# Reordering the gated merge of a hybrid S5, sparse-attention and SwiGLU block, and splitting its 16 weight pieces earlier

## The chip, the cores and the metric

The kernel runs on one core of a Trainium2 chip. The metric is the device time of one execution in microseconds (us). Its engines in the profile are PE (matmuls), DVE, ACT and POOL (elementwise work), and SP, which issues the transfers; every engine runs its instructions in the order in which they were written for it, and waits for another engine on semaphores.

## The reference

One decoder block over 2048 tokens of width 1024, in float32, cut to what matters here:

```python
h = _rms(x, norm1_g)
u, q, k, v, qi, ki, wi, gates = split(h @ w_in)
y_ssm = _s5_branch(u, ..., w_glu, b_glu)       # 512 wide, ends in a gated linear unit
y_att = _dsa_branch(q, k, v, qi, ki, wi)       # 512 wide: each query attends to its 256 best keys
g_ssm, g_att = split(gates)                    # 1024 wide each
merged = sigmoid(g_ssm) * (y_ssm @ w_proj_ssm) + sigmoid(g_att) * (y_att @ w_proj_attn)
x = x + merged @ w_out
h2 = _rms(x, norm2_g)
x = x + (silu(h2 @ w_ffn_gate) * (h2 @ w_ffn_up)) @ w_ffn_down
```

## The kernel before

Every operand of a large product is held as two parts, hi and lo: hi is the value cast to the matmul's reduced type (fp32r), lo is what the cast lost. `mm3` forms hi·hi, hi·lo and lo·hi, three matmuls for one. Parts are made in two steps: a cast (ACT mostly) and a subtraction (POOL or DVE; a split of a weight piece of 128x1024 is "raw" to "ww" in the trace, hi first).

**Stages.** The projections of phase 1 come first. Then three streams run interleaved: *state* (the S5 scan, then `glu`, its gated linear unit), *attention* (for 4 tiles of 128 queries at a time, a search by bisection for the 256 best keys in `topk`, on DVE and ACT, then scores, softmax and values in `attention`), and *dense* (the rest of the gate projections, "gps" in the trace, then four blocks of 512 tokens). The search for the tiles of the next attention group runs on DVE beside the dense block of the group before. Its result goes out as "bias<-fin", and the group's first matmuls are "lg<-kk,q".

**Who comes next** is settled when the program is written out, not on the chip. Each stream is a generator that yields what it needs next; a planner (`Pace`) holds an estimated clock per engine, adds a cost for each instruction (`note`), and takes the first stream whose need is met by PE's estimated clock (`pick`). `spare` gives an elementwise operation to POOL or DVE, whichever the estimate has free sooner; the additions and subtractions of the merge go through it. So the order on every engine is a fixed list, and an edit of one stream moves instructions of all.

**A dense block** (`block`, 512 tokens) does, in this order:

1. The merge: 16 products of 12 matmuls, one for each of 8 groups of 128 output channels (ct) and each branch (br 0 state space, br 1 attention): "f<-act,ww", with act0 the state-space branch's output and act1 the attention's. In the order ct by ct, both branches beside each other. DVE multiplies each by its gate (`scalar_tensor_tensor`, "g<-g,f"), POOL adds the two branches ("g<-g,g"), ACT and DVE make the parts ("mg<-g", "mg<-g,mg").
2. w_out: "f<-ww,mg", 192 matmuls, each group of 24 over all 8 channel groups of mg; then the residual sum into x1.
3. The norm, transposes ("f<-ident,..."), the up and gate products ("f<-h,ww") and the down products ("f<-wd,at").

**Weights** come through `Rings` in pieces of 128x1024, 4 slots of ring "w". In block 0 a piece is loaded raw, split on the spot and its two parts stored to DRAM ("wc<-ww", 1 MB); blocks 1 to 3 load the stored parts ("ww<-wc", 1 MB). Pieces 0 to 7 hold the two projections, one ct of both branches each; pieces 8 to 15 hold w_out; then come those of the feed-forward part. The merge frees a piece after its second product (`drop`), which lets the next load be issued. Gates come back from DRAM ("g<-gate") two channel groups ahead.

**Start of a block.** Block tb begins when the attention of its four tiles is done (`attended >= 4 * (tb + 1)`), and the first one also not before the gates are done (`gated`). A block takes 3 PSUM banks and borrows spare ones in between (`lend`); the last one, which runs alone, takes 8.

## Time and profile before

| | us |
|---|---|
| median of 3 runs (3353.09 to 3363.12) | 3360.59 |
| profiled execution | 3357.88 |
| its span, from first to last instruction | 3355.8 |
| PE busy | 3171.5 (95%) |
| DVE busy | 2106.4 (63%) |
| ACT busy | 1275.1 (38%) |
| POOL busy | 638.1 (19%) |

In a timeline row come first the start and the length of a run of like instructions, then engine and line, the operation, out<-in by the program's names, the count, and in brackets how long the engine sat idle just before and what ended that. All work of an engine is recorded in one helper, so each row has line 206 and is told apart by its names. A row of the groups has the count, then the shortest, median and longest duration in ns.

### The profile page before, as it was taken

How to read it: one execution, taken by the hardware profiler on the slowest of the kernel's cores; microseconds unless marked ns; L12 is line 12 of the kernel's file. 1: busy time of each engine (PE TensorE's matmuls, PEld its weight loads, DVE VectorE, ACT ScalarE, POOL GpSimd, SP SyncE). 2: the span in 40 equal slices, each digit the busy share in tenths (PEclk: the TensorE clock that was granted, in tenths of full speed). 3: DMA queues.
4: the chain of work that ended last, by engine and by line, in shares of the span. 5: the costliest groups of instructions: out<-in, count | busy, mean ns of one | idle time of the engine just before them, and what ended most of it. 6: DMA issues, size and time to landing. Idle time of an engine off the chain costs nothing. (4 is left out here: it accounts for less than half of the span.)

```text
span 3355.8 us, 42712 instructions
## 1 busy us (share of the span) xinstructions
PE 3171.5 (95%) x15528; PEld 2651.1 (79%) x15528; DVE 2106.4 (63%) x4532; ACT 1275.1 (38%) x2211; POOL 638.1 (19%) x628
## 2 busy tenths in 40 slices
PE   7999989899977999989999999999999999999999
PEld 6988767678755788877778888877888888788887
DVE  6555685555587766688687775876886666422223
ACT  3231544445552444346322443665314444210000
POOL 4323676522223311234100000001000000000000
PEclk9999999999988999999999999999999999999999
DMA  5743333534447775656847324366555332755543
GB/s 184 227 122 109 121 89 108 164 120 142 129 166 268 283 257 196 237 182 225 332 187 262 109 93 166 140 236 242 197 213 182 119 108 88 268 195 219 207 177 149
DMA packets 312961, 605.56 MB, mean 180 GB/s; under 512 B 46352, under 2 KB 194608, under 8 KB 282032
## 3 DMA queue, kind: packets, MB, share of 16 engines
q1 hardware_dynamic: 312752, 602.85, 51.7%
q8 instruction: 122, 2.00, 0.2%
q14 instruction: 87, 0.71, 0.1%
HBM read 434.70 MB, written 166.89 MB: 179 GB/s over the span
## 5 line engine op out<-in xcount | busy, mean ns | idle before, releaser
L206 PE MATMUL f<-h,ww 128*128 128x512 f32 (+1 forms) x4416 | 1013.1, 384 | 1.3 <-DVE h L206 0.8
L206 PEld LDWEIGHTS f<-h,ww 128*128 128x128 f32 x4416 | 803.4, 191 | 156.5 <-DVE h L206 1.8
L206 PE MATMUL f<-wd,at 128*128 128x512 f32 x2112 | 518.2, 397 | 28.7 <-DVE t L206 6.5
L206 PEld LDWEIGHTS f<-wd,at 128*128 128x128 f32 x2112 | 396.3, 191 | 116.5 <-DVE t L206 8.1
L206 PE MATMUL gps<-hT,gw 128*128 128x512 f32 x1536 | 387.5, 403 | 4.6 <-ACT gsg L206 3.2
L206 ACT ACTIVATE jka<-S,tr 128x1920 bf16<-128x1920 f32 (+6 forms) x217 | 305.6, 1408 | 180.5 <-DVE tr L206 128.7
L206 PEld LDWEIGHTS gps<-hT,gw 128*128 128x128 f32 x1536 | 288.3, 193 | 68.5 <-ACT gsg L206 5.2
L206 PE MATMUL mm<-w,hT 128*128 128x512 f32 (+1 forms) x1152 | 282.8, 403 | 10.3 <-DVE hT L206 7.2
L206 DVE TENSOR_TENSOR x<-f,x 128x512 f32<-128x512 f32 x352 | 235.1, 686 | 77.0 <-PE f L206 76.4
L206 PEld LDWEIGHTS mm<-w,hT 128*128 128x128 f32 x1152 | 241.5, 239 | 36.7 <-DVE hT L206 8.6
L206 DVE TENSOR_TENSOR tl<-pt,th 128x512 fp32r<-128x512 f32 (+1 forms) x288 | 183.8, 658 | 120.9 <-ACT th L206 119.8
L206 DVE SCALAR_TENSOR_TENSOR t<-t,f 128x512 f32<-128x512 f32 (+1 forms) x123 | 82.1, 668 | 271.8 <-PE f L206 223.6
L206 ACT CAST th<-pt 128x512 fp32r<-128x512 f32 (+1 forms) x288 | 155.5, 563 | 223.8 <-PE pt L206 220.2
L206 PE MATMUL f<-act,ww 128*128 128x512 f32 x768 | 191.8, 411 | 29.5 <-POOL ww L206 20.4
L206 PEld LDWEIGHTS f<-act,ww 128*128 128x128 f32 x768 | 151.2, 199 | 69.5 <-POOL ww L206 24.2
L206 POOL TENSOR_TENSOR g<-g,g 128x512 f32<-128x512 f32 x31 | 39.8, 1285 | 793.9 <-DVE g L206 793.9
L206 PE MATMUL f<-ww,mg 128*128 128x512 f32 x768 | 180.3, 397 | 10.6 <-ACT ww L206 7.0
L206 ACT ACTIVATE P<-P,m 128x1024 f32<-128x1024 f32 (+7 forms) x192 | 172.3, 900 | 46.9 <-DVE m L206 46.8
L206 PE MATMUL lg<-kk,q 128*128 128x512 f32 (+1 forms) x640 | 183.3, 388 | 3.5 <-DMA kk<-kk 3.5
L206 ACT ACTIVATE t<-f 128x512 f32<-128x512 f32 (+1 forms) x92 | 52.9, 575 | 343.8 <-PE f L206 343.7
L206 PEld LDWEIGHTS f<-ww,mg 128*128 128x128 f32 x768 | 147.2, 192 | 43.2 <-ACT ww L206 7.9
L206 ACT CAST at<-t 128x512 fp32r<-128x512 f32 (+1 forms) x92 | 55.2, 600 | 325.4 <-DVE t L206 325.3
(361 smaller groups left out, 4497.9 us busy)
## 6 DMA issues: line engine op xcount, KB each, us to landing
ww<-wc SPq DMA_DIRECT2D x180, 1024.0 KB, 4.9
wd<-wc SPq DMA_DIRECT2D x66, 1024.0 KB, 7.2
wc<-ww SPq DMA_DIRECT2D x60, 1024.0 KB, 7.5
raw<-in_w_in_dram SPq DMA_DIRECT2D x104, 256.0 KB, 3.4
wc<-wd SPq DMA_DIRECT2D x22, 1024.0 KB, 6.3
x<-in_x_dram SPq DMA_DIRECT2D x32, 512.0 KB, 5.3
gate<-gsg SPq DMA_DIRECT2D x64, 256.0 KB, 2.2
g<-gate SPq DMA_DIRECT2D x64, 256.0 KB, 5.7
```

Of the source, the lines that this page charges most:

```text
L206: return f(*args, **kw)
```

## The change

1. `weights`: pieces 0 to 3 hold two channel groups each of the state-space projection, pieces 4 to 7 of the attention's, in place of both branches of one channel group. The first 16 pieces (8 of the projections, 8 of w_out; `EARLY`) are marked as stored parts in block 0 too.
2. `presplit`, a new stream beside `glu`: it loads these 16 raw pieces, splits them (cast on ACT into "pw", subtraction on POOL) and stores the parts, two raw and two pw buffers. `dense` waits for both streams (`ahead`) where it waited for the gates alone.
3. The merge runs all 8 state-space products first and keeps each, times its gate, in the rows of x1, which are not in use yet; then the 8 attention products, each multiplied by its gate, added to what was kept, and split. The block starts without the attention of its own tiles; the wait for it stands ahead of the attention half. The attention branch is loaded after 6 products if it is ready by then, or after 8. The rows of x are loaded when the attention half has used the kept values. Gates are loaded two channel groups ahead within one branch.
4. Blocks take 3 banks each and borrow 5 when all attention is done; the number of down-weight buffers is fixed inside the block.

On PE, the merge and w_out of block 0, before (the state-space branch is act_9338, the attention branch act_9375):

```order
L206 MATMUL gps<-hT,gw 128x512 x330
L206 MATMUL f<-act_9338,ww 128x512 x24
L206 MATMUL f<-act_9375,ww 128x512 x24
L206 MATMUL f<-act_9338,ww 128x512 x12
L206 MATMUL f<-act_9375,ww 128x512 x12
L206 MATMUL f<-act_9338,ww 128x512 x12
```

and of the change (act_9365 and act_9573):

```order
L207 MATMUL u<-yp,uw_7548 128x256 x12
L207 MATMUL gps<-hT,gw 128x512 x282
L207 MATMUL f<-act_9365,ww 128x512 x96
L207 MATMUL f<-act_9573,ww 128x512 x96
L207 MATMUL f<-ww,mg 128x512 x192
```

The twelve groups of 12 that alternated have become two runs of 96, and 48 matmuls of the gates moved ahead of the last one of `glu` ("u<-yp").

On SP, the transfers from the last gate of the gate projections on, before:

```order
L206 DMA gate_0_164<-gsg 128x512 x2
L206 DMA raw<-in_w_proj_ssm_dram 128x4x128
L206 DMA raw<-in_w_proj_attn_dram 128x4x128
L206 DMA act_9338<-act_182 128x2x512 x4
L206 DMA raw<-in_w_proj_ssm_dram 128x4x128
L206 DMA raw<-in_w_proj_attn_dram 128x4x128
L206 DMA g_9373<-gate_0_134 128x512
L206 DMA act_9375<-att_186 128x2x512 x4
L206 DMA g_9380<-gate_0_136 128x512
```

and the last loads of the state-space half of the change (wc_190 to wc_205 are the stored parts; act_9365 and wc_190 to wc_194 were issued ahead of these rows):

```order
L207 DMA g_9508<-gate_0_144 128x512
L207 DMA ww<-wc_195 128x2048
L207 DMA g_9544<-gate_0_146 128x512
L207 DMA g_9569<-gate_0_148 128x512
L207 DMA ww<-wc_196 128x2048
L207 DMA act_9573<-att_186 128x2x512 x4
L207 DMA g_9578<-gate_0_150 128x512
```

The raw loads are gone from here, and the attention branch's load, which stood behind one gate, stands behind the eighth gate of the state-space half (g_9569), whose buffer is that of the sixth.

On DVE, the end of the state-space half of block 0 of the change (H, jkd, cnt, uf and tf are the search's; g_9569 is the eighth gate, g_9578 the first of the attention half; 43 rows of search stand between them, of which the last four are shown):

```order
L207 TENSOR_SCALAR jkd<-H_8777,tf_8127 128x384
L207 SCALAR_TENSOR_TENSOR jkd,cnt_8126<-H_8777,tf_8127,jkd 128x384
L207 TENSOR_SCALAR uf_8128<-cnt_8126 128x2
L207 SCALAR_TENSOR_TENSOR tf_8127<-uf_8128,tf_8127 128x2
L207 SCALAR_TENSOR_TENSOR g_9578<-g_9578,f 128x512
L207 TENSOR_TENSOR mg<-g_9578,mg 128x512
L207 SCALAR_TENSOR_TENSOR g_9580<-g_9580,f 128x512
L207 TENSOR_TENSOR mg<-g_9580,mg 128x512
```

Before, DVE had two products' gates to one split of mg, and search rows between them; now gate and split strictly alternate through the eight attention products, and the search is collected ahead of and behind them.

The diff, cut to its core:

```diff
+EARLY = 16
@@ weights
-        for ct in range(KD):
-            items.append(("w", lambda raw, ct=ct: [
...
+        for w in ("w_proj_ssm", "w_proj_attn"):
+            for c0 in range(0, KD, 2):
+                items.append(("w", lambda raw, w=w, c0=c0: [
...
-        return [(kind, parts, copy, tb > 0) for tb in range(NB) for (kind, parts), copy in zip(items, copies)]
+        return [(kind, parts, copy, tb > 0 or i < EARLY) for tb in range(NB)
+                for i, ((kind, parts), copy) in enumerate(zip(items, copies))]
+    def presplit(self, items, rp, wp):
+        nc, at, idle = self.nc, self.pace.at, self.pace.idle
+        todo, raws = deque(items), deque()
+        def load():
+            if todo:
+                kind, parts, copy, _ = todo.popleft()
+                raw = rp.tile([128, 1024], F32, name="raw")
+                for view, src in parts(raw):
+                    nc.sync.dma_start(view, src)
+                raws.append((raw, copy))
+        load()
+        load()
+        for _ in items:
+            raw, copy = raws.popleft()
+            yield idle("ACT", raw, wp.free_at("pw"))
+            w = wp.tile([128, 2, 1024], F32R, name="pw")
+            nc.scalar.copy(w[:, 0], raw)
+            yield idle("POOL", w)
+            nc.gpsimd.tensor_tensor(w[:, 1], raw, w[:, 0].bitcast(F32), op=ALU.subtract)
+            load()
+            yield at("SP", w)
+            nc.sync.dma_start(copy, w.bitcast(F32))
@@ block
-                    act += [self.load_branch(bigp, br, tb) for br in range(len(act), 2)]
+                    if not act:
+                        act.append(self.load_branch(bigp, 0, tb))
...
-                    for q, (ct, br) in enumerate([(0, 0), (1, 0), (0, 1), (1, 1)] +
-                                                 [(ct, br) for ct in range(2, KD) for br in range(2)]):
-                        w = ld.get("w", 1 if q == 1 else 0)
...
+                    kept = x1.rearrange("p t (a c) -> p (t a) c", a=2)
+                    for q in range(2 * KD):
+                        br, ct = q // KD, q % KD
+                        if q == KD:
+                            if self.attended < 4 * (tb + 1):
+                                yield lambda: at("PE") if self.attended >= 4 * (tb + 1) else ("PE", 1e9, None)
+                            if self.attended == NT:
+                                self.pace.BIAS = 0.0
+                                self.spare_banks = 5
+                        if q == KD - 2 or q == KD:
+                            if len(act) == 1 and self.attended >= 4 * (tb + 1):
+                                act.append(self.load_branch(bigp, 1, tb))
+                            if q < KD:
+                                load_gate(0, 1)
+                                load_gate(1, 1)
+                        w = ld.get("w")
...
+                        x = gates.pop((ct, br))
+                        if br == 0:
+                            nc.vector.scalar_tensor_tensor(kept[:, ct], x, 1.0, ps, op0=ALU.add, op1=ALU.mult)
+                        else:
+                            nc.vector.scalar_tensor_tensor(x, x, 1.0, ps, op0=ALU.add, op1=ALU.mult)
+                            spare(x).tensor_tensor(x, x, kept[:, ct], op=ALU.add)
+                            self.split(x, mg[:, 0, ct], mg[:, 1, ct], nc.scalar, spare(x))
+                        load_gate(ct + 2, br)
+                        if ct % 2 == 1:
                             ld.drop("w")
...
+                            if br == 1:
+                                t = ct // 2
+                                nc.sync.dma_start(x1[:, t], a["x"][0, t0 + t * 128:t0 + (t + 1) * 128])
@@ run
-            yield from self.glu()
+            with ExitStack() as st:
+                pools = self.pool(st, "pr", 2), self.pool(st, "pw", 2)
+                yield from self.pace.among([self.glu(), self.presplit(self.items[:EARLY], *pools)])
+            self.ahead = True
...
-                yield lambda: self.pace.at("PE") if self.gated else ("PE", 1e9, None)
+                yield lambda: self.pace.at("PE") if self.ahead else ("PE", 1e9, None)
...
-                    yield lambda: self.pace.at("PE") if self.attended >= 4 * (tb + 1) else ("PE", 1e9, None)
...
+                    if self.attended < 4 * tb:
+                        yield lambda: self.pace.at("PE") if self.attended >= 4 * tb else ("PE", 1e9, None)
```

More of the change, by code (lines that the diff above doesn't have):

```diff
@@ L372, in __init__ @@
         self.spare_banks, self.lent = 0, False
+        self.ahead = False
         self.dram = ctx.enter_context(tc.tile_pool(name="scr", bufs=1, space=DRAM))
@@ L1665, in weights @@
         items = []
-        for ct in range(KD):
-            items.append(("w", lambda raw, ct=ct: [
-                (raw[:, i * 512:(i + 1) * 512].rearrange("p (k c) -> p k c", k=4),
-                 a[w][0, :, ct * 128:(ct + 1) * 128].rearrange("(k p) c -> p k c", p=128))
-                for i, w in enumerate(("w_proj_ssm", "w_proj_attn"))]))
+        for w in ("w_proj_ssm", "w_proj_attn"):
+            for c0 in range(0, KD, 2):
+                items.append(("w", lambda raw, w=w, c0=c0: [
+                    (raw[:, i * 512:(i + 1) * 512].rearrange("p (k c) -> p k c", k=4),
+                     a[w][0, :, (c0 + i) * 128:(c0 + i + 1) * 128].rearrange("(k p) c -> p k c", p=128))
+                    for i in range(2)]))
         for half in range(2):
@@ L1693, in load_branch, with block @@
         return z
-    def block(self, tb, bigp, ld, nps, nd):
+    def block(self, tb, bigp, ld):
         nc, a, at = self.nc, self.a, self.pace.at
@@ L1760, in block @@
                             ld.tick()
-                        x = gates[ct, br]
-                        nc.vector.scalar_tensor_tensor(x, x, 1.0, ps, op0=ALU.add, op1=ALU.mult)
-                        if br == 1:
-                            ld.drop("w")
-                            x0, x = gates.pop((ct, 0)), gates.pop((ct, 1))
-                            spare(x0).tensor_tensor(x0, x0, x, op=ALU.add)
-                            self.split(x0, mg[:, 0, ct], mg[:, 1, ct], nc.scalar, spare(x0))
-                            load_gate(ct + 2, 0)
-                            load_gate(ct + 2, 1)
+                        x = gates.pop((ct, br))
[7 more added lines that the diff above has]
+                        if ct % 2 == 1:
+                            ld.drop("w")
+                            if br == 1:
+                                t = ct // 2
+                                nc.sync.dma_start(x1[:, t], a["x"][0, t0 + t * 128:t0 + (t + 1) * 128])
                         if q == 3:
                             self.pace.tight = False
-                        if q in (4, 6, 8, 10):
-                            t = q // 2 - 2
-                            nc.sync.dma_start(x1[:, t], a["x"][0, t0 + t * 128:t0 + (t + 1) * 128])
                 fn = self.pool(sm, "fn", 1)
@@ L1862, in block @@
             tp = self.pool(st, "ft", 2)
+            nd = 2 if self.attended == NT else 1
             ld.ring("d", self.pool(st, "fd", nd), nd, 2)
@@ L1980, in dense @@
                 first = ExitStack()
-                ld = Rings(self, self.pool(first, "fraw", 2), 1, self.weights())
+                ld = Rings(self, self.pool(first, "fraw", 2), 1, self.items)
                 self.act = [self.load_branch(bigp, 0, 0)]
@@ L1988, in dense @@
                         first.close()
-                    yield lambda: self.pace.at("PE") if self.attended >= 4 * (tb + 1) else ("PE", 1e9, None)
-                    alone = self.attended == NT
-                    if alone:
-                        self.pace.BIAS = 0.0
-                    yield from self.block(tb, bigp, ld, *((8, 2) if alone else (3, 1)))
+                    if self.attended < 4 * tb:
+                        yield lambda: self.pace.at("PE") if self.attended >= 4 * tb else ("PE", 1e9, None)
+                    yield from self.block(tb, bigp, ld)
+        self.items = self.weights()
         st = ExitStack()
```

6 lines of the change are left out of this document (2 added, 4 removed).

## The prediction, made before the change was run

> **What bounds the kernel now.** I read the page first, then PE's timeline around the place that the change touches.
>
> ```profile
> PE 3171.5 (95%) x15528; PEld 2651.1 (79%) x15528; DVE 2106.4 (63%) x4532; ACT 1275.1 (38%) x2211; POOL 638.1 (19%) x628
> ```
>
> PE is busy 95% of the span of 3355.8. No matmul is added or removed, so only its idle time (3355.8 - 3171.5 = 184 us) and its clock can be won. This is PE from the end of the gate products through block 0's merge and w_out to the next attention group:
>
> ```profile
> 954.65 16.61 PE L206 MATMUL gps<-hT,gw 128*128 128x512 f32 x72 [1.59 <-ACT gsg L206]
> 980.81 5.53 PE L206 MATMUL f<-act,ww 128*128 128x512 f32 x12 [9.54 <-POOL ww L206]
> ...
> 1111.44 1.03 PE L206 MATMUL f<-ident,ha 128*128 128x128 f32 x8
> ...
> 1152.69 0.85 PE L206 MATMUL lg<-kk,q 128*128 128x512 f32 x4
> ...
> 1621.93 43.68 PE L206 MATMUL f<-act,ww 128*128 128x512 f32 x192
> 1665.45 43.68 PE L206 MATMUL f<-ww,mg 128*128 128x512 f32 x192
> ```
>
> The gates end at 971.26 (954.65 + 16.61). Merge and w_out, 384 matmuls, run from 980.81 to 1111.44: 130.6 us. The same 384 in block 1 (last two rows) run without a gap in 87.2 (1621.93 to 1709.13), 2.73 us for a product of 12. Block 0 loses 43.4. PE's waits from 972 to 1130, then two stretches (length, busy us and count of PE, PEld, DVE, ACT, POOL, granted clock, DMA share, GB/s):
>
> ```profile
> PE f L206 <- POOL ww L206: 23.9, 11, 9.5
> PE f L206 <- ACT ww L206: 11.8, 5, 4.6
> ...
> 981.00:1056.00 75.00, 55.18 (x192) 40.23 (x192) 53.50 (x113) 17.38 (x26) 30.49 (x17) 0.86 0.86 295
> 1056.00:1111.00 55.00, 48.68 (x191) 38.94 (x192) 40.49 (x73) 16.55 (x23) 20.32 (x10) 0.89 0.72 260
> ```
>
> Waits for split weights are 35.7 us; without the 9.5 ahead of 981 that is 26 of the 43.4. The rest goes with a clock of 0.86 to 0.89.
>
> **Part 1, the head of block 0.** A split costs a cast and a subtraction; a stored piece costs one load. The merge's own work is in the next rows:
>
> ```profile
> L206 POOL TENSOR_TENSOR ww<-raw,ww x43: 2347/2398/3362, 978.4 to 1562.6; 128x1024 fp32r<-128x1024 f32 x43
> L206 ACT CAST ww<-raw x43: 1031/1047/1059, 986.6 to 1557.1; 128x1024 fp32r<-128x1024 f32 x43
> L206 DVE SCALAR_TENSOR_TENSOR g<-g,f x64: 678/687/691, 987.3 to 2942.3; 128x512 f32<-128x512 f32 x64
> L206 POOL TENSOR_TENSOR g<-g,g x31: 1262/1287/1293, 999.1 to 2943.1; 128x512 f32<-128x512 f32 x31
> ww<-wc SPq DMA_DIRECT2D x180, 1024.0 KB, 4.9
> ```
>
> PE still starts near 981, since the first branch's load stands where it stood and the first stored part lands with it. The waits for ww should vanish: the state-space half would end near 1005 (8 x 2.73 = 21.8, at a clock of 0.9). Then three other waits come up.
>
> (a) The attention branch's load stands on SP behind the eighth gate, whose buffer comes free with the sixth product, near 981 + 6 x 2.73 + 1 = 998; it would land from 1009 on (it took 4 to 10 us from issue in block 3, below), so PE waits some 4 to 11 us.
>
> (b) DVE now runs 43 rows of search between the eighth gate and the first of the attention half. One round of six such rows takes 2.49 us undisturbed:
>
> ```profile
> 964.72 0.30 DVE L206 TENSOR_SCALAR jkd<-H,tf 128x320 bf16<-128x320 uint16 x1
> ...
> 967.21 0.30 DVE L206 TENSOR_SCALAR jkd<-H,tf 128x320 bf16<-128x320 uint16 x1
> ```
>
> Some six rounds are 15 us, so the first attention product is multiplied near 1005 + 4 + 15 = 1024. PE has 7 banks and goes on meanwhile.
>
> (c) From there gate and split strictly alternate on DVE, and a gate's buffer is freed only by the split. One step of block 3 and one reload of block 1:
>
> ```profile
> 2905.96 0.69 DVE L206 SCALAR_TENSOR_TENSOR g<-g,f 128x512 f32<-128x512 f32 x1 [0.28 <-PE f L206]
> 2908.74 0.69 DVE L206 TENSOR_TENSOR mg<-g,mg 128x512 fp32r<-128x512 f32 x1 [2.09 <-ACT mg L206]
> ...
> 1653.12 0.69 DVE L206 TENSOR_TENSOR mg<-g,mg 128x512 fp32r<-128x512 f32 x1 [2.12 <-ACT mg L206]
> ...
> 1659.89 1.31 DVE L206 SCALAR_TENSOR_TENSOR g<-g,f 128x512 f32<-128x512 f32 x2 [0.97 <-DMA g<-gate]
> ```
> ```profile
> 1653.84 0.80 SPq L206 DMA_DIRECT2D g<-gate  x2
> ```
>
> From gate to end of split is 3.47 us (2905.96 to 2909.43), two steps in a row 6.9. The split freed its gate's buffer at 1653.81, and the reloaded gate was used at 1659.89, 6.1 us later. With two buffers to a branch, two products now cost 3.47 plus that reload. The fastest gate landed in 2.5 us, the median in 5.7:
>
> ```profile
> DMA to landing us min/median/max: 2.5/5.7/8.5
> ```
>
> In the attention half the same bytes go out over more time than in block 1 (0.94 of the queue, below), so I take 4.5, between the two, a cycle of 8 us for two products (from 6.0 to 9.6), where PE needs 5.46. The last split ends at 1024 + 3 x 8 + 6.9 = 1055. w_out begins with 48 matmuls for two rows of tiles and needs the last channel group from the 43rd on, 9.6 us after its start; it can start at 1045 and ends at 1089, or 1092 at a clock of 0.95. That wins 20 us of 1111.44, from 14 (reloads of 6.1, clock 0.9) to 26.
>
> (d) What PE wins it must be able to keep: the next group's scores need the search's result, issued here:
>
> ```profile
> 1128.76 4.97 SPq L206 DMA_DIRECT2D bias<-fin  x2
> ```
>
> In the new order the search is six rounds further back when the block begins, 15 us, and 4.5 feed-forward products, 12 us, stand ahead of the first score. PE would be there at 1152.69 + 12 - 20 = 1145. Against the 15 us stands what POOL no longer costs DVE:
>
> ```profile
> 1002.33 2.47 DVE L206 TENSOR_SCALAR jkd<-H,tf 128x320 bf16<-128x320 uint16 x1
> ```
> ```profile
> 1002.34 2.35 POOL L206 TENSOR_TENSOR ww<-raw,ww 128x1024 fp32r<-128x1024 f32 x1
> ```
>
> This search step takes 2.47 us beside a POOL subtraction and 0.30 without (above). Of 51 us of POOL work (30.49 + 20.32) the 8 additions stay, 10 us. I let the search win 7 to 12 back, so that it ends 3 to 8 us later than before; with up to the 19 us that lay between its result (1133.73) and the first score, the scores are ready between 1146 and 1161. PE may wait 0 to 16; I keep 16 of the 20.
>
> **Part 2, the splits beside glu.** 16 casts (17 us) go to ACT, 16 subtractions (38 us) to POOL, 8 MB in and 16 MB out to the queue. The last stretch of the gates:
>
> ```profile
> 935.00:971.50 36.50, 34.55 (x150) 27.61 (x148) 33.65 (x121) 26.17 (x47) 6.91 (x6) 1.00 0.19 66
> ```
>
> POOL (6.91 of 36.50) and DMA (0.19) have room, ACT some. DVE is full (33.65), and a dozen subtractions beside the search could stall it for 2.2 each, 26 us. PE waits here only 1.6 at a time. I take +3: between 0 (all hidden by gate products) and 12 (half the stalls reach PE).
>
> The Trainium skill, "GPSIMD Engine Reference", section "8. Key points", says that GpSimd shares its SBUF interfaces with VectorE and contends with VectorE's operations in a two-port mode or with two SBUF inputs. The trace agrees (2.47 us against 0.30). By that rule the stalls are moved beside glu and not removed, which is the second rival.
>
> **Part 3, blocks 1 to 3.** Blocks 1 and 2 had no gap in the merge (43.68, above; the stretch of it in block 1 is next).
>
> ```profile
> 1620.00:1665.00 45.00, 45.00 (x201) 37.24 (x199) 17.20 (x30) 7.50 (x11) 9.02 (x7) 1.00 0.94 362
> ```
>
> With (c)'s cycle the last split ends 2.9 + 3 x 8 + 6.9 = 33.8 us after the attention half's start, and w_out needs it at 21.8 + 9.6 = 31.4: 2.4 lost, and 2 more because the state-space gates too (0.7 + 5.2 for two products, at the median 0.7 + 5.7) run behind PE's 5.46. I take +4.5 each, from 0 (reload 2.8) to 10 (reload 6.1).
>
> Block 3:
>
> ```profile
> 2886.81 1.97 PE L206 MATMUL lg<-r,hsel 8*128 8x128 f32 x8 [1.78 <-DVE r L206]
> 2888.71 8.25 PE L206 MATMUL f<-act,ww 128*128 128x512 f32 x24
> 2898.07 0.96 PE L206 MATMUL f<-act,ww 128*128 128x512 f32 x3 [1.12 <-DMA act<-att]
> ...
> 2904.28 37.94 PE L206 MATMUL f<-act,ww 128*128 128x512 f32 x159 [0.36 <-DMA act<-att]
> 2942.06 43.69 PE L206 MATMUL f<-ww,mg 128*128 128x512 f32 x192
> ```
> ```profile
> 2893.90 2.50 SPq L206 DMA_DIRECT2D act<-att  x4
> ```
>
> Three of the state-space products now come ahead of the last attention work and fill a wait of 1.8, but the load of the attention branch is issued only behind the eighth, near 2909, and its slices come 4.2 to 10.4 us later (2893.90 to 2898.07 and 2904.28). The ninth product ends at 2920, the last split at 2920 + 24 + 6.9 = 2951, just when w_out needed it before (2942.06 + 9.6). +1, from -3 to +6.
>
> **Sum**, against the profiled execution: 3357.88 - 16 + 3 + 9 + 1 = 3354.9. That execution lies 2.7 under the median of the runs shown; by the median it would be 3357.6. I say 3356, and count the rivals from 3359, the middle of 3357.88 and 3360.59.
>
> **Rivals.** *Full gain* (chance 0.2): reloads of 3 us and a search that ends in time. Head 26, blocks 1 to 3 nothing lost, glu hidden: 3359 - 26 - 3 = 3330. For it: PE's 35.7 us of waits are real, and the chain after 1126 is full. Against: the search rows that now stand in front of the chain.
>
> *Bound by the search* (0.15): half of part 2's stalls, 13 us, reach the search against the 10 it wins back, so that its result comes 15 + 13 - 10 = 18 us later, at 1152, and with 10 us for storing and loading it PE's first score can run at 1162. That is 3 us ahead of 1165 (1152.69 + 12), the place without any gain: 3359 - 3 + 9 + 1 = 3366. For it: DVE at 33.65 of 36.5. Against: part of the 16 subtractions falls beside the scan, ahead of this search.
>
> *Slower by the gate reloads* (0.25): each gate takes the 6.1 us of block 1, in all four blocks. Then every second product waits, 9.6 a cycle: 10 us lost in blocks 1 and 2, 6 in block 3, and block 0 wins 14, less 8 beside glu: 3359 + 20 + 6 - 14 + 8 = 3379. It decides from reloads of about 5.5 us on. For it: the median of 5.7. Against: those were measured with the queue 0.94 full in the merge of block 1.
>
> **How the numbers follow.** Forecast 0.40, rivals 0.20, 0.15 and 0.25. The forecast's own range is 3343 to 3369. With the rivals, 3328 to 3382 leaves out 2 in 10. A measurement here can tell about 0.3%, 10 us. Faster by more (under 3350.5): all of the first rival, 0.17 of the forecast, 0.01 of the second: 0.38. Within: 0.21 + 0.10 + 0.04 = 0.35. Slower: 0.02 + 0.04 + 0.21 = 0.27.
>
> **What would show it.** Right: PE's waits for ww gone between 981 and 1111; w_out of block 0 ending 14 to 26 us earlier; DVE waiting for gates ("<-DMA g<-gate") in the second half of each merge; PE waiting for mg (a split) in w_out of blocks 1 and 2 for 2 to 7 us; one wait for the attention branch in blocks 0 and 3. Wrong: PE waiting for lg's or the search's operands near 1150, PE waits of over 6 us beside glu, or no wait for mg in blocks 1 and 2.

## The result, and the profile after

The kernel became slower: 3395.02 us median (3392.72 to 3399.27) against 3357.55 for the kernel before on the same chip, a ratio of 1.0112 [1.0092, 1.0133], or +37.5 us. The range of the prediction ended at 3382. The profiled execution took 3399.27, its span is 3397.1 (before 3355.8). It was the slowest of four, so the traces lie 41.3 us apart where the medians lie 37.5 apart.

The first page row below is PE's busy time of the kernel after; the three others are its groups of PE that the change touches (count, busy us, mean ns, idle just before them and what ended most of that).

```profile
PE 3176.4 (94%) x15528; PEld 2655.7 (78%) x15528; DVE 2107.0 (62%) x4537; ACT 1279.7 (38%) x2216; POOL 627.5 (18%) x618
...
L207 PE MATMUL gps<-hT,gw 128*128 128x512 f32 x1536 | 390.0, 405 | 11.8 <-ACT gsg L207 10.7
...
L207 PE MATMUL f<-act,ww 128*128 128x512 f32 x768 | 184.1, 402 | 33.6 <-DMA ww<-wc 17.2
...
L207 PE MATMUL f<-ww,mg 128*128 128x512 f32 x768 | 183.4, 401 | 19.4 <-DMA ww<-wc 13.5
```

The same three groups of the kernel before:

```profile
L206 PE MATMUL gps<-hT,gw 128*128 128x512 f32 x1536 | 387.5, 403 | 4.6 <-ACT gsg L206 3.2
...
L206 PE MATMUL f<-act,ww 128*128 128x512 f32 x768 | 191.8, 411 | 29.5 <-POOL ww L206 20.4
...
L206 PE MATMUL f<-ww,mg 128*128 128x512 f32 x768 | 180.3, 397 | 10.6 <-ACT ww L206 7.0
```

PE does the same matmuls, 4.9 us slower, and is idle 220.7 us instead of 184.3. The waits for splits (POOL ww, ACT ww) are gone. In their place stand waits for the stored parts (DMA ww<-wc), and the gate products wait for ACT. PE's timeline after, from the end of the gates through block 0, then the merges of blocks 1 and 3:

```profile
977.82 5.73 PE L207 MATMUL gps<-hT,gw 128*128 128x512 f32 x24 [0.23 <-ACT gsg L207]
1000.75 24.86 PE L207 MATMUL f<-act,ww 128*128 128x512 f32 x96 [17.21 <-DMA ww<-wc]
1031.67 4.18 PE L207 MATMUL f<-act,ww 128*128 128x512 f32 x9 [6.06 <-DMA act<-att]
1036.31 20.52 PE L207 MATMUL f<-act,ww 128*128 128x512 f32 x87 [0.46 <-DMA act<-att]
1056.66 5.60 PE L207 MATMUL f<-ww,mg 128*128 128x512 f32 x24
1068.20 39.95 PE L207 MATMUL f<-ww,mg 128*128 128x512 f32 x168 [5.93 <-DMA ww<-wc]
...
1170.17 1.22 PE L207 MATMUL lg<-kk,q 128*128 128x512 f32 x2 [5.13 <-DMA kk<-kk]
...
1636.79 43.81 PE L207 MATMUL f<-act,ww 128*128 128x512 f32 x192 [0.51 <-DVE x L207]
1680.44 2.88 PE L207 MATMUL f<-ww,mg 128*128 128x512 f32 x12
1684.03 3.00 PE L207 MATMUL f<-ww,mg 128*128 128x512 f32 x12 [0.70 <-DMA ww<-wc]
1692.95 39.86 PE L207 MATMUL f<-ww,mg 128*128 128x512 f32 x168 [5.92 <-ACT mg L207]
...
2950.20 1.62 PE L207 MATMUL f<-act,ww 128*128 128x512 f32 x3 [8.84 <-issue]
...
2984.42 40.91 PE L207 MATMUL f<-ww,mg 128*128 128x512 f32 x168 [3.50 <-DMA ww<-wc]
```

From these marks, and the same ones of before, the 41.3 us of the span divide as follows:

| stretch | predicted | measured |
|---|---|---|
| to the end of the gates (971.26, now 983.55) | +3 | +12.3 |
| from there to the first product of block 0 (9.5, now 17.2) | 0 | +7.7 |
| merge and w_out of block 0 (130.6, now 107.2) | -20 | -23.4 |
| from there to block 1 | +4 | +18.3 |
| merge and w_out of blocks 1, 2, 3 | +4.5, +4.5, +1 | +8.8, +5.2, +10.2 |
| between and after these blocks | 0 | +2.2 |

In block 3 three state-space products now run ahead of the last attention work, so its stretch begins earlier, and 2.8 of its 10.2 us are won back in the last row. Block 0 won what was forecast. The 20 us ahead of it, the 18 behind it and the 24 of the later blocks are to be explained.

**Ahead of block 0.** The cascade beside glu that ends in the longest wait of the gate products, engine by engine:

```profile
914.40 2.81 POOL L207 TENSOR_TENSOR pw<-raw,pw 128x1024 fp32r<-128x1024 f32 x1 [14.58 <-ACT pw L207]
...
919.97 2.33 POOL L207 TENSOR_TENSOR pw<-raw,pw 128x1024 fp32r<-128x1024 f32 x1
914.86 4.01 DVE L207 COPY H<-S 128x640 bf16<-128x640 bf16 x2
918.80 1.23 DVE L207 TENSOR_SCALAR un<-cnt 128x2 int32<-128x2 f32 x1
920.06 2.25 DVE L207 SCALAR_TENSOR_TENSOR tr<-un,tr 128x2 int32<-128x2 int32 x1
922.67 1.15 ACT L207 ACTIVATE jka<-S,tr 128x1024 bf16<-128x1024 f32 x1 [5.09 <-DVE un L207]
924.98 0.58 ACT L207 ACTIVATE gsg<-gps 128x512 f32<-128x512 f32 x1
925.61 30.28 PE L207 MATMUL gps<-hT,gw 128*128 128x512 f32 x120 [6.38 <-ACT gsg L207]
```

POOL works from 914.40 to 922.30 without a gap, on two early subtractions with two rows of gate weights between them. Beside it DVE's two copies of H take 4.01 us (1.0 in the kernel before, and in *no_sub* below), a step of two elements 1.23 us (0.17 undisturbed), and the next one 2.25, until the subtraction on POOL ends (both at 922.3). The search's counts on ACT wait 5.09 for these three rows, and the gate's activation is queued behind the counts, so its PSUM bank comes free late: PE waits 6.38. The prediction had counted stalls of DVE, but no queue behind DVE. The Trainium skill, "SBUF — State Buffer", section "SBUF: two separate sides", says that a DVE instruction with two SBUF inputs (or in a two-port mode) and a GpSimd instruction take a shared port pair as a lock for a whole instruction, and that the other engine blocks until it ends; the trace agrees, the last step, which has two inputs, takes 0.16 us undisturbed and took 2.25.

Of the 12.3 us, the gate products' waits for ACT are 7.5 (10.7 instead of 3.2). Most of the rest is in glu's own products ("u<-yp"), whose waits for DVE and ACT grew from 11.9 to 16.3.

**The first product.** Two things make it later. SP stands at the store of the last gate until ACT has made that gate, and ACT begins on it at 986.84, 3.3 us after PE's last gate product, since rows of the search stand ahead of it on ACT; the loads of block 0 are queued behind that store:

```profile
983.50 4.26 SPq L207 DMA_DIRECT2D gate<-gsg  x2
987.86 2.55 SPq L207 DMA_DIRECT2D act<-act  x4
990.45 3.19 SPq L207 DMA_DIRECT2D ww<-wc  x4
```

Before, ACT began on the last gate at 971.31, right at PE's end, and block 0's loads were issued from 972.34 on. That is some 3 of the 7.7 us. Then four pieces of 1 MB, the state-space branch and gates are loaded at once, and PE starts when the first piece lands, 10.3 us after its issue. The issues of 985 to 1002, with count, size and median time to landing:

```profile
ww<-wc SPq DMA_DIRECT2D x4, 1024.0 KB, 12.6
act<-act SPq DMA_DIRECT2D x4, 512.0 KB, 6.7
```

Over the whole run the median of such a piece is 4.9 us.

**Blocks 1 to 3.** The end of block 1's merge on SP and DVE (ct 4 and 5 are split by the two DVE rows):

```profile
1682.70 0.69 DVE L207 TENSOR_TENSOR mg<-g,mg 128x512 fp32r<-128x512 f32 x1 [2.12 <-ACT mg L207]
...
1686.11 0.69 DVE L207 TENSOR_TENSOR mg<-g,mg 128x512 fp32r<-128x512 f32 x1 [2.12 <-ACT mg L207]
```
```profile
1683.41 3.74 SPq L207 DMA_DIRECT2D g<-gate  x2
1687.24 0.38 SPq L207 DMA_DIRECT2D ww<-wc  x1
...
1688.19 0.38 SPq L207 DMA_DIRECT2D ww<-wc  x1
```

The seventh and eighth gate go into the buffers that these splits free; SP issues the first at 1683.41 and stands at the second until the split of ct 5 ends at 1686.80. Behind it in SP's queue waits the third piece of w_out (1687.24), though PE had been done with its slot near 1675 (w_out's start less two products of 2.73). PE needs it at w_out's 25th matmul, which starts at 1692.95, 5.7 us after that issue. The profile names ACT's last cast there; it ended 0.1 us earlier by chance: in block 3 the same wait ends 6.2 us after the third piece's issue, and PE goes on (2984.42) before the last cast has even started (2984.75).

**Between blocks 0 and 1.** The first of the `un` steps on DVE of the search for the next group (80 of them, over some 196 us in both kernels; other rounds follow), before, then the same step and the last issue of the search's result after:

```profile
820.92 0.15 DVE L206 TENSOR_SCALAR un<-cnt 128x1 int32<-128x1 f32 x1
```
```profile
873.58 0.14 DVE L207 TENSOR_SCALAR un<-cnt 128x1 int32<-128x1 f32 x1
...
1155.07 0.88 SPq L207 DMA_DIRECT2D bias<-fin  x1
```

The result came at 1155 instead of 1133.4, 22 us later; PE's first scores wait 5.9 us for kk, loaded behind it. Of the 18.3 us, PE idles 10.4; in the other 7.9 it does the same matmuls more slowly. One stretch, before and after, then the after's in two parts:

```profile
1170.00:1300.00 130.00, 130.00 (x692) 110.55 (x691) 87.86 (x180) 61.13 (x107) 21.36 (x9) 1.00 0.73 257
```
```profile
1170.00:1300.00 130.00, 129.05 (x672) 109.13 (x673) 84.52 (x183) 58.60 (x105) 21.17 (x9) 0.97 0.72 257
```
```profile
1170.00:1180.00 10.00, 9.05 (x29) 6.97 (x30) 4.58 (x11) 1.85 (x4) 0.32 (x1) 0.63 1.04 421
1180.00:1300.00 120.00, 120.00 (x645) 102.16 (x644) 79.94 (x173) 56.75 (x101) 20.85 (x9) 1.00 0.70 243
```

In this stretch of the after, PE runs 20 matmuls fewer in 130 us, at a clock of 0.97. All of that lies in the first 10 us, at 0.63, right behind the wait of 5.13 us for kk; from 1180 on the clock is 1.00. So here the lower clock comes with a wait of PE and not on its own.

How much of the 18.3 us is the price of the late result isn't shown. In *wait_start* (below) the result comes at 1159.97, later still, and the same stretch takes 508.7 us, 1.6 less than before; there 88 us of work and waits lie between the end of w_out and the first score, here 62.

### The profile page after: what moved, and what is told of

Read it like the earlier page. It is cut to its first block, busy times and chain, and to the rows that moved or that the text cites. A ratio compares the mean times of both kernels' runs of the same rounds, so it can differ in the third digit from the quotient of the medians.

```text
span 3397.1 us, 42762 instructions
## 1 busy us (share of the span) xinstructions
PE 3176.4 (94%) x15528; PEld 2655.7 (78%) x15528; DVE 2107.0 (62%) x4537; ACT 1279.7 (38%) x2216; POOL 627.5 (18%) x618
## 5 line engine op out<-in xcount | busy, mean ns | idle before, releaser
L207 PE MATMUL gps<-hT,gw 128*128 128x512 f32 x1536 | 390.0, 405 | 11.8 <-ACT gsg L207 10.7
L207 PE MATMUL f<-act,ww 128*128 128x512 f32 x768 | 184.1, 402 | 33.6 <-DMA ww<-wc 17.2
L207 POOL TENSOR_TENSOR g<-g,x 128x512 f32<-128x512 f32 x32 | 41.0, 1280 | 877.1 <-DVE g L207 877.1
L207 PEld LDWEIGHTS f<-ww,mg 128*128 128x128 f32 x768 | 149.1, 195 | 53.0 <-ACT mg L207 12.6
```

The lines of the kernel that those rows point to most:

```text
L207: return f(*args, **kw)
```

## The experiments

Times are medians; ratios are to the kernel before, measured beside each run, with their 95% interval. Diffs are against the kernel after unless another is named.

**1. The two halves of the change apart.** *order_only* keeps the new merge, its piece order and block start, but splits in block 0 as before:

```diff
-EARLY = 16
+EARLY = 0
```

> The new merge order with the new pieces, but no split beside glu: block 0 loads raw pieces and splits them on the spot again. Theory A (the split beside glu costs the time ahead of the first score, the merge order costs 5 to 9 us in each of blocks 1 to 3): the gates end near 971 as before, block 0's head is as long as before (130 us) or a little longer, blocks 1 to 3 lose about 22 us together; 3375 to 3385. Theory B (the merge order causes the whole loss, the early split gains): slower than the change, 3400 or more, since the early split's gain is missing too.

3387.31, 1.0095 [1.008, 1.011]. Theory A's marks held: gates at 968.9, a block 0 that takes 132.7 us to the end of w_out, and 24.8 us lost in blocks 1 to 3. The search's result came at 1144.76, 11 us later than before, although its first `un` step came 3 us earlier (817.5), so the new order alone delays it too. *split_only* is the kernel before with only the early split:

```diff
+EARLY = 16
-        return [(kind, parts, copy, tb > 0) for tb in range(NB) for (kind, parts), copy in zip(items, copies)]
+        return [(kind, parts, copy, tb > 0 or i < EARLY) for tb in range(NB)
+                for i, ((kind, parts), copy) in enumerate(zip(items, copies))]
...
-            yield from self.glu()
+                yield from self.pace.among([self.glu(), self.presplit(self.items[:EARLY], *pools)])
```

> The old merge order and the old pieces, with the 16 pieces split beside glu. Theory A: the gates end near 983, block 0's first product starts near 1000, the search for tiles 4 to 7 comes out some 20 us late, so that the first score cannot run before about 1165; blocks 1 to 3 lose nothing; 3360 to 3375. Theory B: the early split gains 20 to 40 us, 3320 to 3340.

3363.64, 1.0019 [1.0008, 1.0029]. So the new order costs 31 us, the early split 6, and the sum is near the 37.5. That doesn't make them independent: block 0's merge and w_out take 130.6 us before, 132.7 in order_only, 96.2 in split_only and 107.2 in the after. Here is order_only's wait for the attention branch in block 0, longer than the after's 6.06:

```profile
1015.41 4.17 PE L207 MATMUL f<-act,ww 128*128 128x512 f32 x9 [11.19 <-DMA act<-att]
```

and split_only's w_out, which lost nothing in blocks 1 to 3:

```profile
L207 PE MATMUL f<-ww,mg 128*128 128x512 f32 x768 | 175.3, 390 | 1.5 <-DMA ww<-wc 1.5
```

Its gates ended 7.8 us later than before and block 0's w_out, at 1091.37, still 20 us earlier; block 1 began 12.9 us earlier (the search's result came at 1164.42), and the rest went behind it, with 20.0 us idle between blocks 2 and 3 against 12.4.

**2. Is it the third piece?** *piece_first* lets the piece be issued ahead of the gates:

```diff
-                        load_gate(ct + 2, br)
                         if ct % 2 == 1:
                             ld.drop("w")
+                            load_gate(ct + 1, br)
+                            load_gate(ct + 2, br)
```

> The change with one thing moved: at each second product the next weight piece is issued ahead of the next two gates, in place of behind them, so that w_out's third piece waits on SP for the split of channel group 3 in place of 5. If that piece behind the gate reloads is what PE waits for in w_out: it is issued 6 to 7 us earlier, PE's wait ahead of the 25th w_out matmul (5.9, 5.9, 3.3 and 3.5 us in blocks 0 to 3) falls to 0 to 2, and blocks 1 to 3 gain 10 to 15 us together; near 3383. If the last split of mg is what it waits for: the wait stays or moves to the 43rd matmul, gain under 5 us, 3390 to 3395.

3404.28, 1.0143 [1.0123, 1.0163], a miss. The third piece came in time and the wait ahead of the 25th matmul was gone, as the first theory had it, but the wait moved one piece on, to the 37th matmul, since the fourth still stood behind a pair of gates:

```profile
1662.82 8.32 PE L207 MATMUL f<-ww,mg 128*128 128x512 f32 x36
1676.20 37.21 PE L207 MATMUL f<-ww,mg 128*128 128x512 f32 x156 [5.07 <-DMA ww<-wc]
```
```profile
1663.82 3.73 SPq L207 DMA_DIRECT2D g<-gate  x2
1667.60 0.42 SPq L207 DMA_DIRECT2D x<-in_x_dram  x1
1668.12 0.38 SPq L207 DMA_DIRECT2D ww<-wc  x1
```

Most of what it lost against the after lies between the ends of w_out of blocks 2 and 3 (674.0 us, 658.7 in the after), which isn't explained.

*gates_shared* takes no transfer out of the order of SP's waits, but makes the gates wait less: the two rings of two buffers become one of four, the same space.

```diff
-                    gp = self.pool(sp, "mgate", 2)
+                    gp = self.pool(sp, "mgate", 4)
-                    def load_gate(ct, br):
-                        if ct < KD:
-                            gates[ct, br] = gp.tile([128, n], F32, name=f"g{br}")
+                    def load_gate(i):
+                        br, ct = i // KD, i % KD
+                        if i < 2 * KD:
+                            gates[ct, br] = gp.tile([128, n], F32, name="g")
...
-                        load_gate(ct + 2, br)
+                        load_gate(q + 4)
```

> The change with one thing altered: the four gate buffers are one ring for both branches (a gate is loaded four products ahead, not two channel groups of its branch), same space, nearly the same order on PE. On SP the last w_out pieces then stand behind a gate reload that waits for the split of channel group 3, in place of 5. Theory (in the change PE waits in w_out for pieces that SP holds back behind gate reloads, and those wait for splits): the piece loads are issued 6 to 8 us earlier against the merge, PE's idle time in w_out (12.5 in all of block 0's merge and w_out, 6.6, 3.3 and 3.5 us in blocks 1 to 3) falls by 10 or more in sum; 3380 to 3387. Rival (the chain of gate, addition, cast and split on DVE, 3.4 us a product, sets w_out's start): the waits stay, 3390 to 3396.

3375.15, 1.0061 [1.0042, 1.008]. In block 1 the third piece was issued at 1675.91, 9.9 us ahead of its matmul (w_out began at 1680.21, 24 matmuls are 5.6), and the w_out group lost its waits:

```profile
1672.15 3.67 SPq L207 DMA_DIRECT2D g<-gate  x2
1675.91 0.38 SPq L207 DMA_DIRECT2D ww<-wc  x1
```
```profile
L207 PE MATMUL f<-ww,mg 128*128 128x512 f32 x768 | 175.6, 390 | 1.7 <-DMA ww<-wc 1.7
```

That is 17 to 20 us of the 37.5 (by the ratios, by the medians), from one ring, more than the expectation had: the waits in w_out fell by 17.7 us, so the reload held on SP is their cause. In the profiled runs the four merges with w_out became 29.8 us shorter, and 14.4 of that was lost again between the blocks. *order_shared* (this ring and EARLY = 0) says the same of the order alone.

> The same ring of gates with the new merge order and no split beside glu. Theory: 8 to 12 us off the run without the ring (3387), so 3375 to 3380, since blocks 1 to 3 lose it as in the change; what is left over before is the wait for the attention branch in blocks 0 and 3 (about 11 and 9) and the later search. Rival: no difference to 3387.

3368.7, 1.0037 [1.0026, 1.0047]: some 19 us less than order_only. PE still waits 13.8 us ahead of the attention half of block 0. The profile names a search row of DVE there, but the branch's first slice, issued at 1008.61, landed at least 8.3 us later, and PE starts at 1017.11.

**3. What does the split beside glu cost?** *dma_only* drops casts and subtractions and stores the raw piece twice:

```diff
-            nc.scalar.copy(w[:, 0], raw)
-            nc.gpsimd.tensor_tensor(w[:, 1], raw, w[:, 0].bitcast(F32), op=ALU.subtract)
...
+            yield at("SP", raw)
+            nc.sync.dma_start(copy[:, 0], raw)
+            nc.sync.dma_start(copy[:, 1], raw)
```

> The change without the casts and subtractions of the 16 pieces: the raw piece is stored twice in place of its two parts (so the lo part is wrong), with the same bytes loaded and stored. If ACT and POOL work, or POOL's hold on DVE, is what slows glu and the gates: the gates end near 971 to 974, the search starts near 825. If the transfers and the order that the planner makes with them are what slows them: the gates end near 980 or later and the search starts near 860 or later, as in the change (983.55 and 873.58).

3429.74, 1.0219 [1.0199, 1.0239]; the gates ended at 1005.71. It doesn't isolate the engines: each next raw load goes into the buffer that was just stored, and SP stands at it until the stores are done (60.3 us in 15 waits), with the gates' own stores and loads behind. *no_sub* drops only the subtraction and stores hi twice:

```diff
-            nc.gpsimd.tensor_tensor(w[:, 1], raw, w[:, 0].bitcast(F32), op=ALU.subtract)
...
-            nc.sync.dma_start(copy, w.bitcast(F32))
+            nc.sync.dma_start(copy[:, 0], w[:, 0].bitcast(F32))
+            nc.sync.dma_start(copy[:, 1], w[:, 0].bitcast(F32))
```

> The change without the 16 early subtractions on POOL: the hi part is stored twice (so the lo part is wrong), with the casts and the same bytes. If POOL's hold on DVE is what lengthens glu and the gates: gates end near 972 to 976 (983.55 in the change, 971.26 before), and PE's wait for the gates' activation (10.7) falls below 4. If the casts on ACT and the transfers do it: 980 or later.

3380.04, 1.0065 [1.0045, 1.0086]. The gates ended at 971.55, as before, 12 us ahead of the after, with the same bytes moved and the same casts. Waits of the gate products (total us, times, longest) in the after and in no_sub:

```profile
PE gps L207 <- ACT gsg L207: 10.7, 5, 6.4
```
```profile
PE gps L207 <- ACT gsg L207: 3.0, 4, 1.1
```

So POOL's subtractions delay the gates, not the 24 MB that are moved there; *wait_dve* below, where DVE makes them, agrees (971.06). The planner's order shifted too: the first `un` step came at 854.9, and the search's result at 1141.96, 13 us ahead of the after's. So the 15 us are not all POOL's hold.

**4. Fewer pieces, or another place for the search.** *split8* is split_only with EARLY = 8. *third8* is the kernel before with 8 pieces split in a stream of its own:

```diff
-        self.pace.run([state(params), attention(), dense(st, gates)])
+        self.pace.run([state(params), attention(), ahead(), dense(st, gates)])
```

> The old merge order with 8 pieces split beside glu in place of 16, else as with 16. If the cost beside glu goes with the number of pieces: the gates end near 975 (971.26 before, 979.01 with 16), the first product of block 0 starts near 988, the search's last result comes near 1148; the time is 3355 to 3362. If any split beside glu shifts the search behind it: the search starts near 868 as with 16 pieces, and the last result is near 1155 or later; 3360 to 3368.

> The old merge order; 8 pieces (the projections) are split ahead of block 0, and the planner takes these splits as a stream of their own, behind the search and the attention and ahead of the gates, not as part of the stream with glu. If the planner puts the search behind glu because the stream of glu and splits comes first: the search for tiles 4 to 7 starts before 840 (820.92 before, 868.82 with the splits beside glu), its last result is out by 1145 (1133 before, 1164), the gates end by 975, and with half of the head's gain (10 to 17 us) the time is 3340 to 3355. If it is the transfers and the engines' work that delay the search: start after 855, 3357 to 3365.

Both are slower than either of their theories had. split8: 3381.37, 1.0073 [1.0052, 1.0095]; the gates ended at 970.80 and block 0's w_out 20.3 us earlier than before, and by block 1 0.6 of that was left. So 8 pieces cost more than 16, and why is open. third8: 3386.62, 1.0087 [1.0069, 1.0106]; the first `un` step of its search came at 842.63, 31 us earlier than the after's and 26 earlier than split_only's (868.82), and its result at 1163.01, 8 us later than the after's and 1.4 earlier than split_only's. An earlier start of these steps on DVE thus gives no earlier result by itself; why is open. *search_first* put the attention stream ahead in the planner's list (`[attention(), state(params), dense(st, gates)]`).

> The change with the planner's list of streams in another order: attention with its search ahead of the state stream (glu and the early splits), so that the search for tiles 4 to 7 stands ahead of all of glu's rows on DVE. If the search's late start (873.58 against 820.92) is what makes the first score of that group late: the search starts by 825, its last result is out by 1135 (1155.07 in the change) and PE's idle time between w_out of block 0 and the first score falls from 13.6 to about 6; glu gets later in turn, gates end 985 to 995; 3385 to 3395. If the result is set by DVE's load behind it: result still after 1148.

3490.46, 1.0394 [1.0373, 1.0415]. The search's result came 140 us earlier than the after's (1014.54), but glu and the early splits moved behind it, and the first product of block 0 came at 1083.59, 83 us later. So it gives no price for the search's lateness alone.

**5. The head of block 0.** *head_first* is gates_shared with the first piece alone loaded ahead of the branch, the other three behind two gates, and in block 0 the attention branch behind the first four gates. *act1_first* is order_shared with the latter alone.

```diff
+                    load_gate(1)
+                    if tb == 0:
+                        self.rest()
+                    for i in range(2, 4):
+                        load_gate(i)
+                    if len(act) == 1 and self.attended >= 4 * (tb + 1):
+                        act.append(self.load_branch(bigp, 1, tb))
...
-                self.act = [self.load_branch(bigp, 0, 0)]
-                ld.fill()
-                ld.ring("w", wp, 4)
+                ld.ring("w", wp, 1)
+                self.act = [self.load_branch(bigp, 0, 0)]
+                self.rest = lambda: ld.ring("w", wp, 4)
```

> The change with the ring of gates (3375) and block 0's head issued in another order: the first stored piece ahead of act0, the next three pieces behind two gates, and the attention branch right behind the first four gates in place of behind the sixth product. If the head's start is late because four pieces and act0 share the queue (17.3 us from the gates' end to the first product), and the wait in the middle is the late load of the attention branch: start 10 to 13 us behind the gates, no wait for the attention branch in block 0, w_out of block 0 ends 8 to 12 us earlier; the time 3365 to 3372, less than the head's gain if the search's result then bounds the first score.

> The new merge order with the ring of gates and no early split (3368.7), the attention branch of block 0 loaded right behind the first four gates. The wait of 13.8 us in the middle of block 0's merge should go; if PE is the bound behind it: 3355 to 3360, the best of the new order; if DVE and the search are: 3362 to 3368.

head_first: 3359.47, 1.0011 [1.0002, 1.0021], 16 us less than gates_shared and below the expected range. PE idled 1.1 us in block 0's merge and w_out, which ended 25.5 us earlier than before; the start still waits 12.8 us. act1_first: 3367.01, 1.002 [1.0009, 1.003]; the interval overlaps order_shared's, so without the early split this load can't be told to be worth anything. The trace says where it went: the wait ahead of the attention half is gone, and PE waits 9.45 us in the middle of that half for the split of a raw piece (ACT ww). In block 3, head_first keeps the after's early start, and its loss is now the branch's load:

```profile
2915.26 25.06 PE L207 MATMUL f<-act,ww 128*128 128x512 f32 x96 [9.41 <-DMA act<-att]
```

**6. A version that beats both?** *wait_start* is head_first with each block waiting for its own attention, as the kernel before does:

```diff
-                    if self.attended < 4 * tb:
-                        yield lambda: self.pace.at("PE") if self.attended >= 4 * tb else ("PE", 1e9, None)
+                    if self.attended < 4 * (tb + 1):
+                        yield lambda: self.pace.at("PE") if self.attended >= 4 * (tb + 1) else ("PE", 1e9, None)
```

*wait8* is this with EARLY = 8; *wait_dve* has the subtractions of the early split on DVE; *wait_plain* is act1_first with the same wait (no early split). wait_dve also lets the branch be loaded at any of the first products, which changes nothing here, since it has been loaded by then.

> The mended head (ring of gates, loads in the new order; 3359.5), and a block begins only when the attention of its own tiles is done, as before the change. If block 3's idle time in the merge (13.8) comes from the load of the attention branch, issued only when its attention is done and with all eight state-space products used up by then: that load is hidden behind eight products again, idle in block 3's merge falls to 1 to 4, the attention's tail keeps its waits; 3345 to 3352, faster than before. If the early products hid as much as the load costs: 3357 to 3362.

> The same with 8 pieces split early in place of 16 (w_out's are split on the spot). If each early piece costs beside glu (12 us for 16) and gains in the head about as much: within 5 us of the run with 16. If w_out's eight pieces are the dear ones, since they fall beside the search: 5 to 10 us faster than with 16. If the head needs them (its w_out waited for splits before): 5 to 10 us slower.

> The same with 16 pieces, the early subtractions on DVE (1.2 us each, 20 us) in place of POOL (2.4 us each). If POOL's hold on DVE is what costs: gates end 4 to 10 us earlier than with POOL (981.8 with the mended head), and the time is 3 to 8 us less. If DVE's fullness is what counts: the search gets later by the 20 us, the gates end no earlier; same time or up to 10 us more.

> The new merge order with the ring of gates and the early load of the attention branch, blocks begin when their attention is done, no early split (3367.0 with the early begin). If the early begin costs in block 3 here too (4.5 of idle in its merge): 3362 to 3365. If the early split is what the new order needs, it stays over 3360; under 3352 the split would be worth nothing.

wait_start: 3354.03, 0.9986 [0.9977, 0.9995], 4 us faster than the kernel before (3358.19 beside it), between its two expected ranges. Block 3's merge is whole again:

```profile
2889.62 44.26 PE L207 MATMUL f<-act,ww 128*128 128x512 f32 x190
```

wait8: 3381.07, 1.0069 [1.0052, 1.0085], 27 us slower than with 16 pieces and far outside its expectations. Its gates ended 13.6 us earlier (971.21) and its w_out in block 0 3.9 earlier, but block 1 began 15.9 later: PE idled 43.7 us in between, against 30.2 in wait_start, though the search's result came no later (1157.54). Why is open. wait_plain: 3358.86, 1.0002 [0.9992, 1.0011], so the repaired order alone is worth nothing against before. wait_dve: 3357.12, 0.9999 [0.999, 1.0008]. Its gates ended at 971.06 against wait_start's 984.79, so POOL's hold costs 13.7 us there. At the start of block 1, 4.7 of these were left, and at the end none. Its search result came 20 us later than wait_start's:

```profile
1179.59 0.79 SPq L207 DMA_DIRECT2D bias<-fin  x1
```

So the subtractions are paid for on either engine, ahead of block 0 by the gates or behind it. That the later search is what takes the gain away is argued, not shown.

## Why the prediction was wrong, step by step

- *The forecast of the time* was 3356 and a sum of -3 us; measured was +37.5. The likeliest case fell by four terms: the gates (9 us more than forecast), the start of block 0 (8), the stretch behind it (14) and blocks 1 to 3 (14).
- *"PE still starts near 981"* failed. It took the place of the loads for their landing, and put nothing in the sum: the first product came 17.2 us after the gates, not 9.5, some 3 us of it from the store of the last gate ahead of the loads on SP. With one piece alone ahead of the branch it was 12.8 (head_first).
- *Part 2* was mis-sized: the gates ended 12.3 later where the sum had +3, and its upper end of 12 was right. Stalls of 2.2 us were seen, but not that ACT, waiting for the stalled search steps, holds back the gate's activation. no_sub and wait_dve show that the subtractions are the cause.
- *Block 0 itself* came out right, in part by luck. Its merge and w_out take 107.2 us (forecast 108 to 111). The wait for the attention branch was 6.06 (forecast 4 to 11), the search ahead of the first attention gate 12.6 us on DVE (forecast 15), gate and split alternate at 7.1 us for two products (forecast 8). But the last split ended 42.3 us after the state-space half, where the forecast had 50, and a wait of 5.93 us for a weight piece in w_out, which the forecast didn't have, took up most of the difference.
- *(d), the search's result "3 to 8 us later"*, failed: 22. The forecast counted the six rounds around the merge. It missed that this search's steps also stand behind more of glu's rows on DVE (first `un` step at 873.58, not 820.92). How far that makes the end late is not settled: the new order alone gives 11 us (order_only), taking the subtractions out of the after brings the result 13 us forward (no_sub), and third8 moved the start without the end.
- *Part 3* had the right place and the wrong wait. The chain of gate and split was near: in block 1 the last split ended at 1693.56, some 3.5 us after an undelayed w_out would have needed it (1680.44 + 9.6, an estimate from the prediction's own rows), where the sum had 2.4 plus 2 for the first half. Reloads in that block took 3 to 5 us from issue to use, one of them held DVE for 1.46, and the signs "<-DMA g<-gate" were seen. But PE stood 18 matmuls earlier, at the 25th, for the weight piece queued behind the eighth gate on SP, and that wait covered the other. The prediction did name, in (a), the branch's load queued behind the eighth gate of the first half; it left out the piece queued behind the eighth of the second. gates_shared shows it, 17 to 20 us. The 5.2 of block 2 lies near the +4.5; block 1 lost 8.8.
- *Block 3* lost 10.2 in place of 1 (6 at most), or 7.4 with what its earlier start won. PE lost 8.84 us ahead of the attention half, of which the prediction had some 8 (its ninth product starts that long behind the eighth), and 3.50 at the piece, which it had not. No releaser is named for the 8.84, but the branch's first slice, issued at 2946.00, landed 4.1 us later, when PE goes on. That load was issued 4.6 us after the state-space half, not right behind it: it waits for the store of the attention's output, and that store stood on SP behind gates (issued at 2938.46, its first part made by 2929.3).
- *The rivals.* "Slower by the gate reloads" (3379) had the sign and the place, again with reload time in place of SP's queue. "Bound by the search" named a true delay, whose price is open. "Full gain" is refuted: even wait_start, whose block 0 won more, ends 4 us ahead of before.
- *What would show it*: the waits for ww <- POOL did vanish; block 0's w_out ended 3.4 us earlier, not 14 to 26. The signs of "wrong" were all three seen: PE waiting for lg's operand at 1170, over 6 us beside glu, and no wait for mg in blocks 1 and 2 (the one that the profile names in block 1 is the piece's).
- *Open*: the slower matmuls after block 0 (7.9 us), followed to a wait of PE in one stretch only; why 8 early pieces cost more than 16; and why split_only, split8, third8, wait_start, wait8 and wait_dve idle 19.5 to 26.1 us between blocks 2 and 3. These are the kernels with an early split in which a block waits for its own attention. Before idles 12.4, wait_plain, which has no early split, 13.4, and the after 12.2.

## What to carry to other kernels

Before moving a load whose buffer comes free late, list what stands behind it on the issuing engine: the wait of a small reload is charged to the independent 1 MB transfer queued behind it, and a deeper ring in the same space (two of two buffers into one of four) took away 17 to 20 of 37 us. Work moved off one stage lands beside another; follow its stall through every in-order queue until it reaches the engine that bounds, and price what the stage behind can keep. When a stage's weights become plain loads, ask what is issued at the same moment: its first product waits for a load that shares the queue with all of them, and for whatever stands ahead of these loads on the issuing engine.

## What was unexpected of the hardware

- A two-element step on DVE took 2.25 us, to the end of POOL's 2.33-us subtraction, where an undisturbed one takes 0.16; sixteen such subtractions moved the end of PE's gate products by 12 to 13.7 us (no_sub, wait_dve), more than half of it through ACT's queue (7.5 us in the after).
- The same 1 MB load landed in 12.6 us in the median (10.3 to 15.4) with four pieces and the branch in flight, against a median of 4.9 over the run.
- The clock granted over 130 us was 0.97 in the kernel after with PE 129.05 us busy, and 1.00 before. All of it was one stretch of 10 us at 0.63, right behind a wait of 5.13 us; a mean over a long stretch hid that.
